# A gated feed-forward stage on one core: up-projection by seven block products, down-projection summed in PSUM

## The chip, the cores and the metric

The kernel runs on one core of a Trainium2 chip. It is written in Bass with the Tile framework, whose scheduler sets the order of instructions on each engine within the limits of data and buffers. The metric is device time in microseconds (us) of one launch; less is better.

Engines are named as in the profile: PE is TensorE (matmul) and PEld its weight loads, DVE is VectorE, ACT is ScalarE, POOL is GpSimd, SP is SyncE, which issues the DMA transfers. PSUM has 8 banks of 128 x 512 f32 here, given out by two tags: "mm" for products and "tp" for transposes (before the change "tp" serves the down-projection too).

## The reference

One layer of a streaming encoder, for a prompt of 1024 rows and 8 samples of 16 rows: 1152 rows of 1024 features, f32. The first sub-layer (adaLN, attention, spatial gating, output projection) stays as it is up to its last projection. The second is the one that changes:

```python
x = x + gt1 * mixed                             # mixed = (...) @ w_out
h2 = modulate(rms_norm(x, norm2_g), sh2, sc2)   # 1152 x 1024
g, u = jnp.split(h2 @ w_ffn_in, 2, axis=-1)     # w_ffn_in 1024 x 5632, D_FF = 2816
gp = jnp.concatenate([conv_cache, g], axis=1)   # two rows ahead of the prompt (zeros) and of each sample
gc = ffn_conv_b
for j in range(3):
    gc = gc + ffn_conv_w[j] * gp[:, j:j + T]    # causal, by feature
out = (jax.nn.gelu(gc) * u) @ w_ffn_out         # 2816 x 1024
x = x + gt2 * out
new_conv = gp[:, -2:]
```

## The kernel before

Each f32 operand of a matmul is kept as two fp32r parts: hi, a rounded copy written by ACT, and lo, the rest, written by DVE or POOL (`split`, L75). A product takes three matmuls for every 128 of the contraction: hi x hi, hi x lo, lo x hi (`mm3`, L97 to L102, so that L100, L101 and L102 are the lines of nearly all matmuls).

**The projection ahead** (`w_out`, L875): two halves of 512 columns, nine token tiles of 128 rows; each product (mxps, 24 matmuls of 512 columns) is gated by DVE (L886) and added to x by POOL (L887). In the second half each tile is written to DRAM (x1_d) and normalised; after tiles 4 and 7 and, later, 8 three tiles are transposed on PE (h2ps), scaled and shifted, and split into h2T, the feature-major operand: 3 chunks of 384 tokens (`h2_chunk`).

**Up** (`up`, L915): 22 feature blocks f of 128. The weights of a block (1024 x 128 of the gate, as much of the up half) come in eight loads to four tiles and are split (wfi). For each chunk of 384 tokens the gate (gps) takes 24 matmuls of 384 columns, ACT copies it out of PSUM into gp, ACT and DVE compute the convolution and the gelu (gc), the up product (ups) takes 24 more, DVE multiplies gc by it, and gc is split into aTh and aTl.

**Down** (`down`, L959): for each f two loads of 128 x 512 of w_ffn_out (wfo), and for each of nine token tiles and two halves three matmuls of 512 columns into one tp bank (fops), which DVE adds to a sum in SBUF (acc, L973). The last two blocks are taken together (`down_last`, flps), with the gate, the addition of x and the output.

The calls are in the order up(f), down(f-1); the scheduler interleaves both on PE. Staging tiles for weights (wst) are five, split weights (wp) nine.

Of the kernel before, what the change touches and what calls it, by code (L numbers as in the profile page):

```python
# [23 lines left out]
NC = TOK // CH  # L24
DB, DS = 8, 16
# [12 lines left out]
def tile_layer(ctx: ExitStack, tc: tile.TileContext, io):  # L38
# [97 lines left out]
    x1_d = dram.tile([TOK, D], F32, name="x1_d")  # L136
    rel_d = dram.tile([H, 512], F32, name="rel_d")
# [691 lines left out]
    psum_phase(3, 5, 0)  # L829
# [14 lines left out]
    with tc.tile_pool(name="mp", bufs=1) as mp_:  # L844
# [17 lines left out]
        g1p, g1s = stile(D, "g1p"), stile(D, "g1s")  # L862
        for j in range(2):
            gate_rows(1, j, g1p[:, 512 * j:512 * (j + 1)], g1s[:, 512 * j:512 * (j + 1)])
        x1 = [stile(D, f"x1_{t}") for t in range(NT)]
        w_o = io["w_out"][0]
        junk2 = stile(D, "junk2")
        h2T = []

        def h2_chunk(c, pl, *tag):  # L870
            for k in range(KD):
                ps = transpose_k(c, k, x1[3 * c:3 * c + 3], "h2")
                modulate(h2T, c, k, ps, G2, S2, pl, "h2", *tag)

        for blk in range(2):  # L875
            bs = slice(512 * blk, 512 * (blk + 1))
            wo = load_block(w_o, 512 * blk, 512, f"wo{blk}")
            if blk == 1:
                h2T = new_xT("h2T")
            for t in range(NT):  # L880
                xr = mp_.tile([P, 512], F32, tag="xr", name=f"xr{blk}_{t}", bufs=3)
                sp.dma_start(xr, xrows(t)[:, bs])
                ps = mmps(f"mxps{blk}_{t}")
                mm_tok(ps, mT, wo, t, 512)
                gt = g1p if t < NTP else g1s
                dve.tensor_tensor(x1[t][:, bs], ps, gt[:, bs], ALU.mult)  # L886
                pool.tensor_tensor(x1[t][:, bs], x1[t][:, bs], xr, ALU.add)  # L887
                if blk == 1:
                    sp.dma_start(x1_d[t * P:(t + 1) * P, :], x1[t])
                    normalise(x1[t], mp_, junk2, f"x1n{t}")  # L890
                    if t in (4, 7):
                        h2_chunk((t - 4) // 3, mp_)


    wfi = io["w_ffn_in"][0].rearrange("r (a n) -> r a n", a=2)
    wfo = io["w_ffn_out"][0]
    with tc.tile_pool(name="fp", bufs=1) as fp:
        acc = [None] * NT
        glast = fp.tile([P, 512], F32, name="glast")
        ccT = fp.tile([P, 3, P], F32, name="ccT")  # L900
# [12 lines left out]
        glv = glast[:, 0:18 * NF].rearrange("p (r f) -> p f r", f=NF)

        def up(f):  # L915
            w = []
# [4 lines left out]
            aT = (stile(TOK, f"aTh{f}", F32R), stile(TOK, f"aTl{f}", F32R))
            w0, w1, w2, bb = convw[:, 0, f:f + 1], convw[:, 1, f:f + 1], convw[:, 2, f:f + 1], convb[:, f:f + 1]
            prev = None
            for c in range(NC):
# [10 lines left out]
                act.activation(gp[:, 2:2 + npr], gps[:, :npr], AF.Copy)  # L935
                gc = fp.tile([P, CH], F32, tag="gc", name=f"gc{f}_{c}", bufs=4)
                parts = [(gp[:, 0:npr], gp[:, 1:npr + 1], gp[:, 2:npr + 2], gc[:, :npr])]
                if npr < CH:
                    sg = gp[:, npr + 2:npr + 2 + DB * 18].rearrange("p (b s) -> p b s", b=DB)
                    act.activation(sg[:, :, 2:18], gps[:, npr:].rearrange("p (b s) -> p b s", b=DB), AF.Copy)  # L940
                    dve.tensor_copy(sg[:, :, 0:2], ccv[:, f, :, :])
                    parts.append((sg[:, :, 0:16], sg[:, :, 1:17], sg[:, :, 2:18], gc[:, npr:].rearrange("p (b s) -> p b s", b=DB)))
                    dve.tensor_copy(glv[:, f, 0:2], gp[:, npr:npr + 2])
# [12 lines left out]
        def load_down(f):
            return [load_w(wfo[f * P:(f + 1) * P, hf * 512:(hf + 1) * 512], [512], f"wfo{f}_{hf}") for hf in range(2)]

        def down(f, aT):  # L959
# [4 lines left out]
            for t in range(NT):
                ts_ = slice(t * P, (t + 1) * P)
                for hf in range(2):
                    hs = slice(512 * hf, 512 * (hf + 1))
                    ps = tpps(f"fops{f}_{t}_{hf}")
                    mm3(ps, [(aT[0][:, ts_], aT[1][:, ts_], w[hf][:, 0, :], w[hf][:, 1, :])])
                    if f == 0:  # L970
                        dve.tensor_copy(acc[t][:, hs], ps)
                    else:
                        dve.tensor_tensor(acc[t][:, hs], ps, acc[t][:, hs], ALU.add)  # L973

        def gate_acc():

            g2 = []
            gpt = stile(D, "g2p")
            for j in range(2):
                gp = gpt[:, 512 * j:512 * (j + 1)]  # L980
                gs = fp.tile([P, 512], F32, name=f"g2s{j}")
# [98 lines left out]
```

## Time and profile before

| | us |
|---|---|
| median of 3 runs (lowest, highest) | 1732.83 (1732.26, 1732.91) |
| the profiled execution: its time | 1734.26 |
| its span, first to last instruction | 1732.5 |
| PE busy in it | 1697.4 |
| DVE, ACT, POOL busy | 934.8, 585.8, 266.5 |
| mean granted clock of PE | 0.994 of full speed |

Busy time counts each instruction from its start to its end, with overlaps counted once. Matmuls overlap: the next one starts before the last has drained, so that the mean duration of one is longer than what it adds to a dense sequence. Idle time is put down to what ended it. Rows of the form "L973 DVE TENSOR_TENSOR acc<-fops,acc 128x512 ... x342" are groups: line, engine, operation, output and inputs, shape, count, then busy time and mean ns of one.

### The profile page before, as it was taken

Reading aid. Unit: us, or ns where it says so; the run is one execution under the profiler, and the core shown is the slowest. Engines: PE = TensorE matmul, PEld = TensorE weight load, DVE = VectorE, ACT = ScalarE, POOL = GpSimd, SP = SyncE. Lnnn points to the kernel's source line nnn. Section 1 sums busy time; section 2 is a strip of 40 time slices with the busy share of each in tenths; the row PEclk is TensorE's granted clock in tenths of the full one; section 3 lists DMA queues with packets and bytes.
Section 4 is the critical chain, followed back from the end, with each engine's and each line's share of the span. In section 5 each row is a group of like instructions: output and inputs, shape, how many; then the busy total and the mean of one; then the engine's idle time right before and its main releaser. Section 6 shows DMA issues by size and latency. Waiting matters only on the chain.

```text
span 1732.5 us, 26462 instructions
## 1 busy us (share of the span) xinstructions
PE 1697.4 (98%) x10244; PEld 1550.0 (89%) x10244; DVE 934.8 (54%) x2011; ACT 585.8 (34%) x1263; POOL 266.5 (15%) x400
## 2 busy tenths in 40 slices
PE   6999999999999999999999999999999999999998
PEld 4798888799998889898889999999999999999997
DVE  4552111137667534472367666556666555666677
ACT  5442111136555534540254222223222223222221
POOL 5410000034224200053351000000000000000063
PEclk9999999999999999999999999999999999999999
DMA  9125444421110133472442111111111111111123
GB/s 352 59 74 165 150 138 142 153 60 33 52 33 17 40 114 106 134 271 72 140 134 66 38 37 42 44 37 45 54 37 37 49 37 37 61 38 37 41 82 150
DMA packets 131090, 147.60 MB, mean 85 GB/s; under 512 B 11544, under 2 KB 101892, under 8 KB 130965
## 3 DMA queue, kind: packets, MB, share of 16 engines
q1 hardware_dynamic: 130965, 145.92, 26.3%
q8 instruction: 80, 1.31, 0.3%
q14 instruction: 45, 0.37, 0.1%
HBM read 123.34 MB, written 24.60 MB: 85 GB/s over the span
## 4 chain that ended last, share of the span: by engine, by line
PE 89%; DVE 4%; DMA 2%; issue 2%; ACT 1%; POOL 1%; DVEq 0%; ACTq 0%; POOLq 0%
PE ups L102 5%; PE ups L100 5%; PE ups L101 5%; PE gps L100 5%; PE gps L102 5%; PE gps L101 5%; PE fops L101 5%; PE fops L100 5%; PE fops L102 5%; PE gbps L102 2%; PE o L686 2%; PE qkps L100 2%; PE gbps L100 2%; PE gbps L101 2%; PE qkps L102 2%; PE qkps L101 2%
## 5 line engine op out<-in xcount | busy, mean ns | idle before, releaser
L973 DVE TENSOR_TENSOR acc<-fops,acc 128x512 f32<-128x512 f32 x342 | 231.7, 687 | 85.1 <-PE fops L102 84.8
L100 PE MATMUL ups<-h2T,wfi 128*128 128x384 f32 x528 | 178.7, 338 | 2.2 <-ACT gp L935 2.2
L101 PE MATMUL ups<-h2T,wfi 128*128 128x384 f32 x528 | 178.3, 338 | 0.0
L102 PE MATMUL ups<-h2T,wfi 128*128 128x384 f32 x528 | 178.2, 337 | 0.0
L102 PE MATMUL gps<-h2T,wfi 128*128 128x384 f32 x528 | 177.3, 336 | 0.4 <-DVE wfi L77 0.4
L100 PE MATMUL gps<-h2T,wfi 128*128 128x384 f32 x528 | 177.4, 336 | 0.0
L101 PE MATMUL gps<-h2T,wfi 128*128 128x384 f32 x528 | 177.0, 335 | 0.0
L935 ACT ACTIVATE gp<-gps 128x384 f32<-128x384 f32 (+1 forms) x66 | 30.1, 456 | 336.2 <-PE gps L102 330.3
L102 PE MATMUL fops<-wfo,aTl 128*128 128x512 f32 x360 | 141.9, 394 | 0.0
L100 PE MATMUL fops<-wfo,aTh 128*128 128x512 f32 x360 | 141.9, 394 | 0.0
L101 PE MATMUL fops<-wfo,aTh 128*128 128x512 f32 x360 | 141.8, 394 | 0.0
L930 POOL MEMSET gp<- 128x2 f32 x22 | 2.1, 99 | 712.7 <-DVE gc L948 712.7
L100 PEld LDWEIGHTS ups<-h2T,wfi 128*128 128x128 f32 x528 | 100.0, 189 | 6.1 <-ACT gp L935 2.5
L102 PEld LDWEIGHTS ups<-h2T,wfi 128*128 128x128 f32 x528 | 99.9, 189 | 5.1
L101 PEld LDWEIGHTS ups<-h2T,wfi 128*128 128x128 f32 x528 | 100.1, 190 | 3.8
L102 PEld LDWEIGHTS gps<-h2T,wfi 128*128 128x128 f32 x528 | 99.2, 188 | 4.4 <-DVE wfi L77 0.8
L100 PEld LDWEIGHTS gps<-h2T,wfi 128*128 128x128 f32 x528 | 99.2, 188 | 3.5
L101 PEld LDWEIGHTS gps<-h2T,wfi 128*128 128x128 f32 x528 | 99.2, 188 | 2.8
L100 PE MATMUL qkps<-wqk,h1T 128*128 128x256 f32 x288 | 83.7, 291 | 0.9 <-ACT qf L580 0.9
L101 PE MATMUL qkps<-wqk,h1T 128*128 128x256 f32 x288 | 82.0, 285 | 0.0
L102 PE MATMUL qkps<-wqk,h1T 128*128 128x256 f32 x288 | 81.9, 284 | 0.0
L102 PEld LDWEIGHTS fops<-wfo,aTl 128*128 128x128 f32 x360 | 67.6, 188 | 15.9
(416 smaller groups left out, 4072.3 us busy)
## 6 DMA issues: line engine op xcount, KB each, us to landing
adaw<-in_w_ada_dram SPq DMA_DIRECT2D x48, 512.0 KB, 4.9
wfi_0s<-in_w_ffn_in_dram SPq DMA_DIRECT2D x44, 128.0 KB, 2.5
wfi_1s<-in_w_ffn_in_dram SPq DMA_DIRECT2D x44, 128.0 KB, 2.7
wfi_2s<-in_w_ffn_in_dram SPq DMA_DIRECT2D x44, 128.0 KB, 2.6
wfi_3s<-in_w_ffn_in_dram SPq DMA_DIRECT2D x44, 128.0 KB, 2.7
wfo_0s<-in_w_ffn_out_dram SPq DMA_DIRECT2D x22, 256.0 KB, 3.2
wfo_1s<-in_w_ffn_out_dram SPq DMA_DIRECT2D x22, 256.0 KB
mb_d<-sgb SPq DMA_DIRECT2D x8, 576.0 KB, 4.2
```

What stands on the lines that cost most here:

```text
L100: pe.matmul(ps, lhsT=ah, rhs=bh, start=(i == 0), stop=False)
L101: pe.matmul(ps, lhsT=ah, rhs=bl, start=False, stop=False)
L102: pe.matmul(ps, lhsT=al, rhs=bh, start=False, stop=(i == n - 1))
L686: pe.matmul(o[hs, :], lhsT=v[:, k0 // P + i, hs], rhs=out[t, x][:, i * P:(i + 1) * P], start=(i == 0), stop=(i == nk - 1))
L930: pool.memset(gp[:, 0:2], 0.0)
L935: act.activation(gp[:, 2:2 + npr], gps[:, :npr], AF.Copy)
L973: dve.tensor_tensor(acc[t][:, hs], ps, acc[t][:, hs], ALU.add)
```

## The change

With the rows of h2 in four blocks of 288 tokens (QB) and the 1024 features of the contraction in two halves, a unit u is two token blocks (a = 2u, b = 2u + 1). The product of a 2 x 2 block matrix of h2 (token block by half of the contraction) and one of the weights (half by gate or up column) is formed from seven block products and not eight (Winograd's form of Strassen's algorithm). Each block product is 4 k x 3 = 12 matmuls of 288 columns:

- operands of a unit: A11, A12, A22 and S1 = A21 + A22, S2 = S1 - A11, S3 = A11 - A21, S4 = A12 - S2;
- weights of a feature block: B11, B21, B22 and T1 = B12 - B11, T2 = B22 - T1, T3 = B22 - B12, T4 = B21 - T2;
- products: A11 B11, S2 T2, S3 T3 and A22 T4 accumulate one after the other in bank X, A12 B21 in Y, S1 T1 and then S4 B22 in Z. ACT copies X out after the first, second, third and fourth product; DVE adds what belongs together.

All operands (7 x 2 units x 4 k, hi and lo) are built before the up stage by `operands`: unit 0 behind token tile 4 of w_out's second half, unit 1 after tile 8. `raw_block` makes a transposed, scaled and shifted block of 288 tokens, alternately on ACT and DVE. POOL and DVE form the sums, ACT and DVE the splits. The weights of each f are loaded in four transfers of 256 KB; POOL forms the T sums, and seven tiles are split where four were.

The gated result is not split and kept, but written to DRAM (aT_d, four transfers for each f). Down is a stage after up: three groups of three token tiles, whose six sums of 128 x 512 stay in six PSUM banks over all 22 f. For every f the group loads and splits a 128 x 384 piece of aT_d and both wfo tiles, so that wfo is loaded three times in all. At a group's end DVE multiplies the banks by the gate, adds x1 (read from DRAM) and SP writes them out. After the attention stage PSUM is given out as six mm banks and two tp banks; it was three and five. The rows xr that w_out adds share the five staging tiles of the weights.

```diff
-    psum_phase(3, 5, 0)
+    psum_phase(6, 2, 0)
...
+    def operands(u, first):
+        at = Slices(u)
+        for k in range(4):
+            a11, a12 = first[k], first[k + 4]
+            a21, a22 = (raw_block(2 * u + 1, kk, "r") for kk in (k, k + 4))
+            s1, s2, s3, s4 = (vtile(f"s{i}_{u}_{k}") for i in range(1, 5))
+            pool.tensor_tensor(s1, a21, a22, ALU.add)
+            dve.tensor_tensor(s2, s1, a11, ALU.subtract)
+            pool.tensor_tensor(s3, a11, a21, ALU.subtract)
+            dve.tensor_tensor(s4, a12, s2, ALU.subtract)
+            for op, src in zip(OPS, (a11, a12, a22, s1, s2, s3, s4)):
+                hi, lo = at.take(), at.take()
+                split(hi, lo, src)
+                opnd[u][op, k] = (hi, lo)
...
+                if t in (2, 6):
+                    first[t // 4] = [raw_block(0 if t == 2 else 2, k, "a") for k in range(KD)]
+                if t == 4:
+                    operands(0, first[0])
...
+        pool.tensor_tensor(t3, b22, b12, ALU.subtract)
+        pool.tensor_tensor(b12, b12, b11, ALU.subtract)
...
+        pool.tensor_tensor(t2, b22, t1, ALU.subtract)
...
+        pool.tensor_tensor(b21, b21, t2, ALU.subtract)
...
+    def unit(f, u, W):
+        ca, cb = 2 * u, 2 * u + 1
+        X, Y, Z = (mmps(f"{n}{f}_{u}", QB) for n in "XYZ")
+        product(X, u, "A11", W["B11"], True)
+        act.activation(x1c, X, AF.Copy)
...
+        product(Y, u, "A12", W["B21"], True)
...
+            dve.tensor_tensor(dst, y, x, ALU.add)
...
+        gca = conv(f, ca, *gate_rows_in(f, ca, sum_in))
...
+        product(X, u, "S2", W["T2"], False)
+        act.activation(u2, X, AF.Copy)
...
+        product(Z, u, "S1", W["T1"], True)
...
+        product(X, u, "S3", W["T3"], False)
+        act.activation(u3, X, AF.Copy)
+        dve.tensor_tensor(upb, Z, u3, ALU.add)
...
+        product(X, u, "A22", W["T4"], False)
...
+        gcb = conv(f, cb, *gate_rows_in(f, cb, copy_in))
+        gated(f, cb, gcb, upb)
...
+        product(Z, u, "S4", W["B22"], False)
+        dve.tensor_tensor(u2, Z, u2, ALU.add)
+        gated(f, ca, gca, u2)
...
+    for g in range(3):
+        ts = range(3 * g, 3 * g + 3)
+        acc = {(t, hf): mmps(f"fops{t}_{hf}") for t in ts for hf in range(2)}
+        for f in range(NF):
+            a = load_w(aT_d[f][:, g * CH:(g + 1) * CH], [CH], f"a{g}_{f}")
+            w = [load_w(wfo[f * P:(f + 1) * P, hf * 512:(hf + 1) * 512], [512], f"wfo{g}_{f}_{hf}") for hf in range(2)]
...
+                        pe.matmul(acc[t, hf], lhsT=a[:, x, o], rhs=w[hf][:, y, :], start=(f == 0 and i == 0), stop=(f == NF - 1 and i == 2))
```

Three places show how the change moves instructions. The first is DVE around the last token tile of w_out (x1_8). Before, weight splits (wfi, L77), one chunk of scaled rows (h2t) and then the first convolution stand there:

```order
L245 TENSOR_SCALAR h2t1_6_9197<-h2ps1_6_9193,G2_83,S2_84 128x384 [waits PE_49,Pool_49]
L77 TENSOR_TENSOR wfi1_1_9358<-wfi1_1s_9355,wfi1_1_9358 128x512 [waits DMAHW1_49,Activation_49]
L886 TENSOR_TENSOR x1_8_8444<-mxps1_8_9211,g1s_8417 128x512 [waits PE_49]
L245 TENSOR_SCALAR h2t1_7_9205<-h2ps1_7_9201,G2_83,S2_84 128x384 [waits Pool_49]
L77 TENSOR_TENSOR wfi1_2_9364<-wfi1_2s_9361,wfi1_2_9364 128x512 [waits DMAHW1_49,DMAHW0_49,Activation_49]
```

After, the rows from x1_8 on are operand splits (L78, op) and sums (s2, s4):

```order
L959 TENSOR_TENSOR x1_8_8472<-mxps1_8_9345,g1s_8445 128x512 [waits PE_49]
L78 TENSOR_TENSOR wB21_0_9401<-b0_10_9394,wB21_0_9401 128x512 [waits DMAHW1_49,Activation_49]
L78 TENSOR_TENSOR op10_9074<-s3_0_0_9057,op10_9074 128x288 [waits Activation_49]
L78 TENSOR_TENSOR op10_9074<-s4_0_0_9058,op10_9074 128x288 [waits Activation_49]
L78 TENSOR_TENSOR op10_9074<-r1_5_9089,op10_9074 128x288 [waits Activation_49]
L935 TENSOR_TENSOR s2_0_1_9092<-s1_0_1_9091,a0_1_8933 128x288 [waits Pool_49]
L937 TENSOR_TENSOR s4_0_1_9094<-a0_5_8957,s2_0_1_9092 128x288 [waits DVE_49]
L919 TENSOR_SCALAR r1_2_9119<-h2ps1_2_9115,G2_83,S2_84 128x288 [waits PE_49]
```

Some hundred rows follow from x1_8 to the sum of Y0_0 (L1083), most of them splits of op.

The second place is PE in the middle of the up stage, feature block 10. Before, one up product follows the gate product, and its first matmul waits for ACT (X_49 in brackets is the semaphore of engine X):

```order
L102 MATMUL gps10_1_12498<-h2T01_8788,wfi10_3_12432 128x384
L100 MATMUL ups10_1_12531<-h2T01_8788,wfi10_0_12414 128x384 [waits Activation_49]
L101 MATMUL ups10_1_12531<-h2T11_8791,wfi10_0_12414 128x384
L102 MATMUL ups10_1_12531<-h2T01_8788,wfi10_0_12414 128x384
L100 MATMUL ups10_1_12531<-h2T01_8788,wfi10_0_12414 128x384
```

After, S3's product into X10_0 (weights wT3) is followed by ten matmuls into X11_0, and A22's product (wT4) goes to the same bank X10_0:

```order
L1028 MATMUL X10_0_12284<-op10_9074,wT3_10_12247 128x288 [waits Activation_49]
L1028 MATMUL X10_0_12284<-op10_9074,wT3_10_12247 128x288 x2
L1028 MATMUL X10_0_12284<-op0_2_9110,wT3_10_12247 128x288 x3
L1028 MATMUL X10_0_12284<-op01_9145,wT3_10_12247 128x288 x3
L1028 MATMUL X10_0_12284<-op11_9176,wT3_10_12247 128x288 x3
L1028 MATMUL X11_0_12558<-op00_9063,wB11_11_12399 128x288
L1028 MATMUL X11_0_12558<-op10_9074,wB11_11_12399 128x288 x3
L1028 MATMUL X11_0_12558<-op0_3_9135,wB11_11_12399 128x288 x3
L1028 MATMUL X11_0_12558<-op01_9145,wB11_11_12399 128x288 x3
L1028 MATMUL X10_0_12284<-op00_9063,wT4_10_12262 128x288 [waits Activation_49]
L1028 MATMUL X10_0_12284<-op00_9063,wT4_10_12262 128x288 x2
```

A bank of one unit is thus written four times, with an ACT copy between, and other units' matmuls stand between.

The third place is SP, which issues the loads. Before, the two wfo loads of a block stand between the loads of wfi for the following ones:

```order
L90 DMA wfi16_3s_14325<-in_w_ffn_in_dram 128x2x128 [waits DMAHW6_49,DVE_49]
L90 DMA wfi16_3s_14325<-in_w_ffn_in_dram 128x2x128 [waits DMAHW7_49]
L92 DMA wfo15_0s_14523<-in_w_ffn_out_dram 128x512 [waits DMAHW0_49,DVE_49]
L92 DMA wfo15_1s_14528<-in_w_ffn_out_dram 128x512 [waits DMAHW1_49,DVE_49]
L90 DMA wfi17_0s_14623<-in_w_ffn_in_dram 128x2x128 [waits DMAHW3_49,DMAHW2_49,DVE_49]
```

After, at the passage from up to down, the writes of the last gated rows (gc to aT_d) and of the convolution's rows (glo) stand between the first loads of the down stage:

```order
L1067 DMA aT_d21_110<-gc21_1_15453 128x288 [waits DMAHW7_49,DVE_49]
L1067 DMA aT_d21_110<-gc21_0_15359 128x288 [waits DMAHW0_49,DVE_49]
L93 DMA a0_0s_15619<-aT_d0_89 128x384 [waits DMAHW1_49,Activation_49,Pool_49]
L93 DMA wfo0_0_0s_15624<-in_w_ffn_out_dram 128x512 [waits DMAHW2_49,Activation_49]
L93 DMA wfo0_0_1s_15629<-in_w_ffn_out_dram 128x512 [waits DMAHW3_49,Activation_49,Pool_49]
L1125 DMA o_cp_dram<-glo_15586 44x128 [waits DMAHW4_49,DVE_49]
L1067 DMA aT_d21_110<-gc21_2_15475 128x288 [waits DMAHW5_49,DVE_49]
L1067 DMA aT_d21_110<-gc21_3_15556 128x288 [waits DMAHW6_49,DVE_49]
L1126 DMA o_cs_dram<-glo_15586 84x128 [waits DMAHW7_49]
L1129 DMA o_cs_dram<-glo_15586 128x128 [waits DMAHW0_49]
L1129 DMA o_cs_dram<-glo_15586 128x128 [waits DMAHW1_49]
L1129 DMA o_cs_dram<-glo_15586 12x128 [waits DMAHW2_49]
```

The second load from aT_d (a0_1s) comes in the next row.

More of the change, by code (lines that the diff above doesn't have):

```diff
@@ L24 @@
 NC = TOK // CH
+QB = TOK // 4
 DB, DS = 8, 16
@@ L136, in tile_layer @@
     x1_d = dram.tile([TOK, D], F32, name="x1_d")
+    aT_d = [dram.tile([P, TOK], F32, name=f"aT_d{f}") for f in range(NF)]
     rel_d = dram.tile([H, 512], F32, name="rel_d")
@@ L860, in tile_layer @@
                 split(mT[0][c][:, j, :], mT[1][c][:, j, :], m)
[L862 to L873, printed above, removed]
@@ L875, in tile_layer @@
-        for blk in range(2):
-            bs = slice(512 * blk, 512 * (blk + 1))
-            wo = load_block(w_o, 512 * blk, 512, f"wo{blk}")
-            if blk == 1:
[L879 to L892, printed above, removed]
@@ new lines, in tile_layer @@
+    g1p, g1s = stile(D, "g1p"), stile(D, "g1s")
+    for j in range(2):
+        gate_rows(1, j, g1p[:, 512 * j:512 * (j + 1)], g1s[:, 512 * j:512 * (j + 1)])
+    x1 = [stile(D, f"x1_{t}") for t in range(NT)]
+    w_o = io["w_out"][0]
+    junk2 = stile(D, "junk2")
+    first = [None, None]
+    for blk in range(2):
+        bs = slice(512 * blk, 512 * (blk + 1))
+        wo = load_block(w_o, 512 * blk, 512, f"wo{blk}")
+        for t in range(NT):
+            xr = staged(f"xr{blk}_{t}")
+            sp.dma_start(xr, xrows(t)[:, bs])
+            ps = mmps(f"mxps{blk}_{t}")
+            mm_tok(ps, mT, wo, t, 512)
+            gt = g1p if t < NTP else g1s
+            dve.tensor_tensor(x1[t][:, bs], ps, gt[:, bs], ALU.mult)
+            pool.tensor_tensor(x1[t][:, bs], x1[t][:, bs], xr, ALU.add)
+            if blk == 1:
+                sp.dma_start(x1_d[t * P:(t + 1) * P, :], x1[t])
+                normalise(x1[t], fp, junk2, f"x1n{t}")
+                if t in (2, 6):
+                    first[t // 4] = [raw_block(0 if t == 2 else 2, k, "a") for k in range(KD)]
+                if t == 4:
+                    operands(0, first[0])
@@ new lines, in product, with gate_rows_in @@
+    def product(ps, u, op, w, begin):
+        n = 0
+        for k in range(4):
+            hi, lo = opnd[u][op, k]
+            ks = slice(k * P, (k + 1) * P)
+            for wj, x in ((0, hi), (0, lo), (1, hi)):
+                pe.matmul(ps, lhsT=w[:, wj, ks], rhs=x, start=(begin and n == 0), stop=(n == 11), skip_group_check=True)
+                n += 1
+    halo = [None]
+    def gate_rows_in(f, c, fill):
+        gp = vtile(f"gp{f}_{c}", NV)
+        if c == 0:
+            pool.memset(gp[:, 0:2], 0.0)
+        else:
+            pool.tensor_copy(gp[:, 0:2], halo[0][:, QB:QB + 2])
+        halo[0] = gp
+        npr = min(QB, SEQ - c * QB)
+        fill(gp[:, 2:2 + npr], 0, npr)
+        sg = None
+        if npr < QB:
+            sg = gp[:, npr + 2:npr + 2 + DB * 18].rearrange("p (b s) -> p b s", b=DB)
+            fill(sg[:, :, 2:18], npr, QB)
+            dve.tensor_copy(sg[:, :, 0:2], ccv[:, f, :, :])
+            dve.tensor_copy(glv[:, f, 0:2], gp[:, npr:npr + 2])
+            dve.tensor_copy(glv[:, f, 2:18].rearrange("p (b j) -> p b j", b=DB), sg[:, :, 16:18])
+        return gp, sg, npr
@@ new lines, in tile_layer @@
+    W = [{} for _ in range(NF)]
+    ws = [up_weights(f, W[f]) for f in range(NF)]
+    for _ in range(2):
+        next(ws[0])
+    operands(1, first[1])
+    for g in ws[0]:
+        pass
+    prev = None
+    for f in range(NF):
+        nxt = ws[f + 1] if f + 1 < NF else iter(())
+        for u in range(2):
+            g = unit(f, u, W[f])
+            for i in range(5):
+                next(g)
+                if prev is not None and i < 2:
+                    next(prev)
+                if u == 1 or i >= 3:
+                    next(nxt, None)
+            prev = g
```

303 lines of the change are left out of this document (159 added, 144 removed).

## The prediction, made before the changed kernel had run

> **What bounds the kernel now.** I read the page first (span, busy shares, the chain of waits), then the timeline of TensorE, its groups by form, and the span cut at the places where TensorE's order changes.
>
> ```profile
> span 1732.5 us, 26462 instructions
> PE 1697.4 (98%) x10244; PEld 1550.0 (89%) x10244; DVE 934.8 (54%) x2011; ACT 585.8 (34%) x1263; POOL 266.5 (15%) x400
> PE 89%; DVE 4%; DMA 2%; issue 2%; ACT 1%; POOL 1%; DVEq 0%; ACTq 0%; POOLq 0%
> ```
>
> TensorE is busy for 98% and carries 89% of the chain that ends last; the other engines have half of their time free. So the price of a matmul decides. Its price is not its duration, since matmuls overlap. The timeline (start, duration) gives it from start to start:
>
> ```profile
> 401.82 0.28 PE L101 MATMUL qkps<-wqk,h1T 128*128 128x256 f32 x1
> 404.45 0.28 PE L102 MATMUL qkps<-wqk,h1T 128*128 128x256 f32 x1
> 841.76 0.39 PE L100 MATMUL mxps<-wo,mT 128*128 128x512 f32 x1
> 847.20 0.39 PE L100 MATMUL mxps<-wo,mT 128*128 128x512 f32 x1
> 911.61 1.25 PE L234 MATMUL h2ps<-ident,x 128*128 128x128 f32 x10
> 1202.19 0.33 PE L100 MATMUL gps<-h2T,wfi 128*128 128x384 f32 x1
> 1206.35 0.34 PE L100 MATMUL ups<-h2T,wfi 128*128 128x384 f32 x1
> ```
>
> The two qkps rows stand 22 matmuls apart: 2.63/22 = 0.1195 us for 256 columns. The mxps rows are 24 apart: 5.44/24 = 0.2267 for 512. The last two are 24 apart: 4.16/24 = 0.1733 for 384. Ten transposes take 1.25, the last of them about 0.27, so 0.109 each. Between 256 and 384 the line gives 0.133 for the new width of 288, which no row has.
>
> ```profile
> 785.30:888.70 103.40, 103.40 (x482) 86.30 (x481) 38.56 (x53) 25.19 (x47) 39.00 (x43) 1.00 0.33 108
> 900.90:903.90 3.00, 0.79 (x4) 0.47 (x3) 0.92 (x2) 0.87 (x2) 0.41 (x4) 0.91 0.77 212
> 903.90:911.00 7.10, 6.50 (x24) 5.83 (x24) 4.30 (x9) 4.26 (x7) 0.00 (x0) 0.56 0.34 85
> 911.00:1683.00 772.00, 772.00 (x4090) 724.64 (x4089) 484.00 (x904) 220.14 (x420) 28.84 (x38) 1.00 0.15 45
> 1683.00:1726.80 43.80, 41.73 (x205) 36.25 (x203) 37.98 (x56) 6.98 (x14) 20.20 (x15) 1.00 0.37 137
> 1726.80:1732.50 5.70, 0.00 (x0) 0.00 (x0) 2.79 (x5) 0.00 (x0) 0.00 (x0) 0.73 0.46 184
> ```
>
> These are busy times and counts by stretch (PE, weight loads, DVE, ACT, POOL, then the granted clock). TensorE is full up to 900.9; then it waits some 2.2 us, runs about 7 us at a granted clock of 0.56, is full again from 911, and leaves a tail of 5.7 after its last matmul. The counts show what is not dense. From 785.3 to 1726.8 (941.5 us) the code issues 3168 matmuls of 384 columns, 432 + 1188 of 512, 79 transposes and 3 last ones of the stage ahead: 549.0 + 367.3 + 8.6 + 0.5 = 925.4 us. So 16 us there are no dense work: 5 at 900.9 to 911, about 2 of idle time after 1683, the rest spread over the alternation of widths.
>
> **The change, part by part.**
>
> *Up-projection.* 3168 x 0.1733 = 549.0 us become 22 x 2 x 7 x 12 = 3696 x 0.133 = 491.6: -57.4. The Trainium skill ("TensorE: Matmul & The Clock Gate", section "Back-to-back issue gap") gives an isolated gap of N/2.4 + 2.5 ns; by it the two would be 514.8 and 452.8, an estimate of -62. The rows, 11 to 13 ns above that gap, decide here.
>
> *Down-projection.* The same 1188 matmuls of 512: nothing. Its 342 adds into acc go, which are not on the path.
>
> ```profile
> L973 DVE TENSOR_TENSOR acc<-fops,acc 128x512 f32<-128x512 f32 x342 | 231.7, 687 | 85.1 <-PE fops L102 84.8
> ```
>
> *Transposes* of the normalised rows: 96 instead of 72 (blocks of 288 rows out of three tiles of 128): 24 x 0.109 = +2.6.
>
> *The losses of before* go with the order that made them and are counted anew below: -14 of the 16 (some may be rounding of the spacings, and 7 are shown idle time).
>
> *Building the operands* is the new work on the path. Each of the 7 operands exists for 2 units and 4 k: 56 splits of 288 into hi (ACT) and lo (DVE), 16 sums on DVE, 16 on POOL. The unit-1 part can start only when the last token tile is normalised.
>
> ```profile
> 1211.41 0.69 DVE L973 TENSOR_TENSOR acc<-fops,acc 128x512 f32<-128x512 f32 x1
> 1212.01 0.68 DVE L77 TENSOR_TENSOR wfi<-wfi_0s,wfi 128x512 fp32r<-128x512 f32 x1
> 1212.61 0.69 DVE L973 TENSOR_TENSOR acc<-fops,acc 128x512 f32<-128x512 f32 x1
> L77 DVE TENSOR_TENSOR aTl<-gc,aTh 128x384 fp32r<-128x384 f32 x66 | 37.2, 563 | 25.4 <-ACT aTh L76 25.4
> 835.25 1.29 POOL L887 TENSOR_TENSOR x<-x,xr 128x512 f32<-128x512 f32 x1 [4.14 <-DVE x L886]
> 835.67 1.43 DVE L77 TENSOR_TENSOR wo<-wo_6s,wo 128x512 fp32r<-128x512 f32 x1 [0.49 <-ACT wo L76]
> L593 POOL TENSOR_TENSOR qk<-qk,kg 128x128 f32<-128x128 f32 x36 | 17.6, 488 | 25.3 <-DVE qk L591 12.7 <-issue 3.7 <-ACT qf L580 3.4
> ```
>
> DVE works 512 columns every 0.60 us (1211.41, 1212.01, 1212.61) with 0.69 for one; 384 take 0.563 alone, so 0.13 less, and 288 about 0.37 apart by the same slope. POOL takes 0.488 for 128 and 1.29 for 512, so 0.82 for 288. In DVE's order after the change a hundred rows stand between the end of the last w_out product and the point from which TensorE has all it needs: 47 splits and 14 sums of 288 (61 x 0.37 = 22.6), 10 weight splits (6.0), and 29 of other kinds (block rows out of PSUM, the last normalise, the sample's rows, the first sum of Y: about 9): 38 us. POOL has 14 sums of 288 and 8 of 512 there, and two small ones: 23.8. The two meet: at 835.67 a split that otherwise takes 0.69 took 1.43 while POOL ran 1.29, 0.57 us lost per us of POOL, so 23.8 x 0.57 = 13.6. DVE also waits in its order for POOL's first sum and ACT's copies at each of 8 steps (0.8 us, one sum, each): 6. That makes 58 us. TensorE has other work for 17.3 of them: six products of f = 0 (72 x 0.133 = 9.6), 22 sets of three transposes (7.2), the transposes of the cache rows (0.5). Loss 58 - 17.3 = 41, and after such a gap the half clock of 903.9 to 911 comes again (24 matmuls in 7.1 instead of 4.2): +3. Together +44. The bounds: 38 us (nothing meets, no waits) gives +24; 75 (POOL wholly in series, 62, and twice the waits) gives +61. I take 58, which rests on the row at 835.67.
>
> The Trainium skill ("SBUF — State Buffer", section "Who interferes with whom") states that a DVE instruction with two SBUF inputs contends with a GpSimd instruction that reads SBUF, through a shared pair that is an exclusive lock. By that rule alone the two times add up, 38 + 24 = 62; the row at 835.67, held up for 0.74 of POOL's 1.29, agrees in kind.
>
> *The steady up stage.* A feature block is 168 x 0.133 = 22.3 us.
>
> ```profile
> L76 ACT ACTIVATE wfo<-wfo_1s 128x512 fp32r<-128x512 f32 x22 | 13.9, 633 | 2.5 <-PE fops L102 2.5
> L935 ACT ACTIVATE gp<-gps 128x384 f32<-128x384 f32 x44 | 21.6, 492 | 270.5 <-PE gps L102 264.7 <-issue 5.8
> L935 ACT ACTIVATE gp<-gps 128x256 f32<-128x256 f32 x22 | 8.5, 384 | 65.6 <-PE gps L102 65.6
> 1206.54 0.38 ACT L935 ACTIVATE gp<-gps 128x256 f32<-128x256 f32 x1 [2.97 <-PE gps L102]
> ```
>
> ACT has 7 weight splits (7 x 0.633), 9 copies out of PSUM (0.41, between 0.384 and 0.492) and 4 conv and gelu pairs: some 12.5 us of 22.3. DVE has the same 7 splits, about 8 conv steps and 10 adds: 14 to 16. Both fit, so throughput costs nothing. New is that X is handed to ACT and taken back three times in each unit. In the order, S3's product into X10_0 is followed by 10 matmuls of another bank (1.33 us), and then A22's product needs X10_0 copied. ACT starts a copy at once when free (1206.54, while the last gps matmul, started at 1206.17, ends at 1206.50): 0.33 for the matmul's end, 0.41 copy, about 0.2 to let go: 0.96 of 1.33. With a weight split (0.63) just begun it is 1.6, late by 0.25. Some such delays in 22 blocks: +5, and +3 for the first blocks after the build. Bounds: 0 and 1 us per block (22). I take the lower side, since the order puts other work ahead of each such wait.
>
> *Up to down.* The first loads of the down stage stand on SP behind the writes of gc21_1 and gc21_0, the second step's behind those of gc21_2, gc21_3 and the cache rows.
>
> ```profile
> wfo_0s<-in_w_ffn_out_dram SPq DMA_DIRECT2D x22, 256.0 KB, 3.2
> o_yp_dram<-acc SPq DMA_DIRECT2D x8, 512.0 KB, 2.6
> GB/s 352 59 74 165 150 138 142 153 60 33 52 33 17 40 114 106 134 271 72 140 134 66 38 37 42 44 37 45 54 37 37 49 37 37 61 38 37 41 82 150
> ```
>
> A load lands 3.2 us after its issue, then a split by ACT (0.63) and DVE (0.69): 4.5 behind the write's issue, of which the last products hide a part: +3 (0 to 8). After that each f of a group of three token tiles has 18 x 0.2267 = 4.08 us of matmuls, for which 0.7 MB must come, 173 GB/s; slices of this trace reached 271 and 352. Five staging buffers at three per step must each be refilled within 5 x 4.08/3 = 6.8 us: 3.2 + 1.3 + the queue, near 5.5. So +3 for three group starts (0 to 10). The gated rows' 88 writes and 22 more pairs of weight loads run on queues that are idle there. Tail: 12 DVE steps and a write as now; 5.7 stays.
>
> **Sum.** -57.4 + 2.6 - 14 + 44 + 8 + 6 = -10.8. The profiled execution took 1734.3 (its span 1732.5 and 1.8 around it), so 1723.5; the median of the runs, 1732.83, is 1.4 below that execution, so 1722.
>
> **Rivals.**
>
> 1. *Hand-overs of X, Y and Z* (the slower side). If ACT or DVE are late at most of the 12 waits of a feature block, each by 0.1 us, a block loses 1.2 instead of 0.2: +22, 1744. From 0.9 us per block (1722 + 22 x 0.67 = 1737) the kernel is slower. For it: three copies in series on one bank, and DVE behind POOL's weight sums; against it: ACT's 44% free. Chance 0.2.
> 2. *The build is better hidden* (38 us instead of 58): 1702, chance 0.12; or *worse* (75): 1739, chance 0.1. For the first, most of POOL's sums may fall where DVE waits anyway; for the second, the split of 1.43 is one instance and queues wait in order.
> 3. *The down stage goes by its loads.* If a refill takes 7.5 instead of 6.8 us, a step takes 4.5: 66 x 0.4 = +26, 1748. For it: loads share queues with the x1 rows; against: 173 GB/s is half of what the first slice moved. Chance 0.08.
> 4. *Narrow matmuls don't get cheaper*, because each one's weight load must fit in:
>
> ```profile
> L101 PEld LDWEIGHTS qkps<-wqk,h1T 128*128 128x128 f32 x288 | 55.1, 191 | 0.3 <-issue 0.2
> ```
>
> A weight load takes 0.191, longer than 0.133; if it set the pace, 3696 x 0.191 = 706, and the kernel would take 1936. But beside that same load the qkps matmuls run every 0.1195. Chance 0.02. The Trainium skill, in the section named first, also says that in a stream of such pairs the spacing is set by both, 81 ns at 128 columns and 131 at 512; between these, as an estimate, 3696 narrow matmuls would cost 14 us more than 3168 wide ones. By that rule the change loses; the mxps rows, 227 ns at 512, contradict it.
>
> **How the numbers follow.** The forecast has 0.48, with a range of its own of 1712 to 1733. A measurement can tell 0.2%, 3.5 us: faster is under 1729.4, slower over 1736.3. Faster: 0.41 of the forecast and 0.12 of the better build, 0.53. Same: 0.07 of the forecast and 0.07 from the near ends of rivals 1 and 2: 0.14. Slower: 0.33. The range from 1704 to 1747 leaves out the far end of the better build, the down stage by its loads, and the narrow matmuls.
>
> **What would show it.** Products in the trace 0.133 us apart; TensorE idle for about 40 us between the last mxps and the second product of unit 1, with DVE full and its 288-column splits near 0.7 while POOL runs; up blocks at 22.5 us; fops 0.2267 apart for 269 us, with less than 1 us at a group's start. Wrong would be the forecast with up blocks above 23.2, with gaps before fops at each f that end with a load, or with an idle stretch under 25 or over 55 us.

## The result

The changed kernel takes 1714.82 us (median of 4 runs, 1712.86 to 1715.73) where the kernel before takes 1732.87 in the same runs: 18.0 us less, ratio 0.9893 with a 95% interval of 0.9876 to 0.991. The profiled execution took 1715.73 with a span of 1714.0, 18.5 below the span before.

The page of the changed kernel, the rows that answer to those of before:

```profile
span 1714.0 us, 28905 instructions
PE 1652.3 (96%) x10796; PEld 1502.5 (88%) x10796; DVE 918.7 (54%) x2013; ACT 721.2 (42%) x1613; POOL 357.5 (21%) x526
PE 89%; DVE 4%; DMA 2%; POOL 1%; ACT 1%; issue 1%; SPq 0%; DVEq 0%; POOLq 0%; ACTq 0%
```

TensorE still carries 89% of the chain. The span cut at the new stages (PE, weight loads, DVE, ACT, POOL, granted clock, DMA):

```profile
786.60:888.40 101.80, 101.80 (x466) 84.24 (x465) 35.12 (x53) 21.47 (x41) 32.82 (x39) 1.00 0.35 111
888.40:945.00 56.60, 30.54 (x139) 23.69 (x137) 48.81 (x97) 28.59 (x68) 30.30 (x26) 0.65 0.14 44
945.00:955.00 10.00, 8.16 (x44) 7.60 (x45) 6.65 (x14) 6.37 (x13) 1.60 (x3) 0.74 0.27 79
955.00:1410.00 455.00, 455.00 (x3437) 455.00 (x3436) 317.18 (x611) 221.92 (x510) 121.67 (x163) 1.00 0.24 73
1410.00:1432.10 22.10, 20.60 (x152) 19.90 (x151) 10.02 (x30) 8.67 (x23) 0.49 (x3) 1.00 0.32 97
1432.10:1442.00 9.90, 7.03 (x24) 4.97 (x23) 5.04 (x12) 3.53 (x7) 0.00 (x0) 0.83 0.51 153
1442.00:1707.10 265.10, 265.09 (x1170) 219.21 (x1168) 137.14 (x224) 108.45 (x193) 0.00 (x0) 1.00 0.64 202
1707.10:1714.00 6.90, 0.00 (x0) 0.00 (x0) 4.00 (x7) 0.00 (x0) 0.00 (x0) 0.82 0.51 197
```

Three things are to be seen. From 955 to 1410 the up stage is dense: 455.00/3437 = 0.1324 us for a matmul of 288 columns. From 1442 to 1707 the down stage is dense too, at 202 GB/s. And between the last w_out product (888.3) and 955 TensorE does little, while DVE is busy for 48.8 of 56.6 us. With each matmul and transpose counted at its dense spacing (0.2267, 0.1324, 0.109 us), TensorE loses 44.3 us from 888.3 to 960, 0.2 from there to 1400, 7.6 from 1400 to 1450, at the passage, and 0.1 in the rest of the down stage. In the kernel before it lost 6.1 where the up stage began and 10.4 behind that.

In the build two waits belong together. The timeline of POOL, DVE and PE (start, duration, idle time ahead and what ended it):

```profile
930.53 4.36 POOL L1004 TENSOR_TENSOR t<-b,b 128x512 f32<-128x512 f32 x1 [5.65 <-DMA b<-in_w_ffn_in_dram]
930.98 0.68 DVE L78 TENSOR_TENSOR wB<-b,wB 128x512 fp32r<-128x512 f32 x1
931.78 0.45 DVE L78 TENSOR_TENSOR op<-s,op 128x288 fp32r<-128x288 f32 x1
934.97 1.26 POOL L1005 TENSOR_TENSOR b<-b,b 128x512 f32<-128x512 f32 x1
936.31 1.26 POOL L1009 TENSOR_TENSOR t<-b,b 128x512 f32<-128x512 f32 x1
937.53 0.79 POOL L934 TENSOR_TENSOR s<-r,r 128x288 f32<-128x288 f32 x1
938.28 1.27 POOL L1013 TENSOR_TENSOR b<-b,t 128x512 f32<-128x512 f32 x1
938.35 1.51 DVE L935 TENSOR_TENSOR s<-s,a 128x288 f32<-128x288 f32 x1 [4.58 <-POOL s L934]
938.85 0.61 PE L1028 MATMUL Z<-op,wT 128*128 128x288 f32 x1 [7.21 <-ACT op L77]
```

POOL takes up three weight sums of the next feature block (L1004, L1005, L1009) ahead of an operand sum (L934). The first of them is held for 4.36 us instead of 1.29 while DVE works through its splits. Then DVE waits 4.58 for the operand sum, and TensorE 7.21 for ACT's split of it. The Trainium skill ("SBUF — State Buffer", section "Who interferes with whom") says that issue order decides which of the two blocks. The rows agree only in part. The sum on DVE at 938.35, which starts behind POOL's of 938.28, took 1.51, where splits of the same size take 0.45. But DVE's splits at 930.98 and 931.78 start behind POOL's sum of 930.53, and they keep their usual 0.68 and 0.45.

### The profile page after: what moved, and what is told of

Read it like the earlier page. It is cut to its first block, busy times and chain, and to the rows that moved or that the text cites. A ratio compares the mean times of both kernels' runs of the same rounds, so it can differ in the third digit from the quotient of the medians.

```text
span 1714.0 us, 28905 instructions
## 1 busy us (share of the span) xinstructions
PE 1652.3 (96%) x10796; PEld 1502.5 (88%) x10796; DVE 918.7 (54%) x2013; ACT 721.2 (42%) x1613; POOL 357.5 (21%) x526
## 4 chain that ended last, share of the span: by engine, by line
PE 89%; DVE 4%; DMA 2%; POOL 1%; ACT 1%; issue 1%; SPq 0%; DVEq 0%; POOLq 0%; ACTq 0%
PE X L1028 16%; PE fops L1170 15%; PE Z L1028 8%; PE Y L1028 4%; PE o L688 2%; PE gbps L103 2%; PE qkps L101 2%; PE gbps L101 2%; PE gbps L102 2%; PE qkps L103 2%; PE qkps L102 2%; PE gaps L101 2%; PE gaps L102 2%; PE gaps L103 2%; PE adaps L382 2%; PE ptp L678 2%
## 5 line engine op out<-in xcount | busy, mean ns | idle before, releaser
L1170 PE MATMUL fops<-wfo,a 128*128 128x512 f32 x1188 | 271.7, 391 | 2.9 <-ACT wfo L77 2.9
L1170 PEld LDWEIGHTS fops<-wfo,a 128*128 128x128 f32 x1188 | 224.0, 189 | 50.4 <-ACT wfo L77 3.9
L1028 PE MATMUL X<-op,wT 128*128 128x288 f32 x1584 | 233.3, 296 | 2.0 <-ACT u L1095 1.5
L1028 PEld LDWEIGHTS X<-op,wT 128*128 128x128 f32 x1584 | 218.7, 189 | 2.9 <-ACT u L1095 2.2
L1028 PE MATMUL Z<-op,wT 128*128 128x288 f32 x528 | 79.8, 298 | 11.0 <-ACT op L77 8.2
L1028 PE MATMUL X<-op,wB 128*128 128x288 f32 x528 | 83.8, 300 | 1.9 <-DVE op L78 1.9
L1028 PE MATMUL Y<-op,wB 128*128 128x288 f32 x528 | 80.3, 299 | 0.2
L1028 PE MATMUL Z<-op,wB 128*128 128x288 f32 x528 | 77.0, 294 | 0.0
L1004 POOL TENSOR_TENSOR t<-b,b 128x512 f32<-128x512 f32 x22 | 31.4, 1428 | 191.0 <-DVE wB L78 177.7
L101 PE MATMUL gaps<-h1T,wga 128*128 128x384 f32 x192 | 66.6, 347 | 0.0
L103 PE MATMUL gbps<-h1T,wgb 128*128 128x384 f32 x192 | 65.9, 343 | 0.0
L102 PE MATMUL gaps<-h1T,wga 128*128 128x384 f32 x192 | 65.1, 339 | 0.0
L101 PE MATMUL gbps<-h1T,wgb 128*128 128x384 f32 x192 | 64.9, 338 | 0.0
```

What stands on the lines that cost most here:

```text
L101: pe.matmul(ps, lhsT=ah, rhs=bh, start=(i == 0), stop=False)
L102: pe.matmul(ps, lhsT=ah, rhs=bl, start=False, stop=False)
L103: pe.matmul(ps, lhsT=al, rhs=bh, start=False, stop=(i == n - 1))
L1004: pool.tensor_tensor(t3, b22, b12, ALU.subtract)
L1028: pe.matmul(ps, lhsT=w[:, wj, ks], rhs=x, start=(begin and n == 0), stop=(n == 11), skip_group_check=True)
L1170: pe.matmul(acc[t, hf], lhsT=a[:, x, o], rhs=w[hf][:, y, :], start=(f == 0 and i == 0), stop=(f == NF - 1 and i == 2))
```

## The experiments

Each kernel ran in turns with the kernel before, so ratios to it are compared. Losses are TensorE's, counted as above.

**The down stage alone (e1).** The up-projection of before, with the new down stage:

```diff
-                split(aT[0][:, cs], aT[1][:, cs], gc)
+                sp.dma_start(aT_d[f][:, cs], gc)
...
+        for f in range(2, NF):
+            run(up(f))
         conv_rows()
+        psum_phase(6, 2, 0)
```

> The up-projection of before (eight block products' worth, 384 columns), its gated rows written to DRAM, and the new down stage behind it. Theory (the seven products gain 60 us and their operands give back about 44; the down stage by itself matters little): before's loss of 16 us beside dense work shrinks by the alternation of widths and the idle time at its end, some 9, and 3.5 at the passage and 1.2 in the tail come new: 1728 us, -3 to -8. Rival (the gain of the change comes from the down stage, from its sums in PSUM and the adds that go): -15 to -18, 1715 to 1718.

Measured: 1723.12 beside 1735.44, ratio 0.9931 (0.9916 to 0.9946), 12 us less. The cut of its span:

```profile
892.90:960.00 67.10, 66.99 (x397) 66.57 (x396) 39.28 (x82) 28.73 (x54) 12.69 (x18) 1.00 0.30 92
960.00:1441.00 481.00, 481.00 (x2777) 481.00 (x2776) 167.43 (x383) 146.67 (x287) 1.79 (x18) 1.00 0.21 66
1441.00:1448.00 7.00, 5.87 (x34) 5.47 (x33) 5.18 (x12) 4.16 (x9) 0.00 (x0) 1.00 0.35 93
1448.00:1716.60 268.60, 268.58 (x1185) 222.11 (x1183) 134.32 (x219) 106.38 (x189) 0.00 (x0) 1.00 0.62 196
1716.60:1723.70 7.10, 0.00 (x0) 0.00 (x0) 3.98 (x7) 0.00 (x0) 0.00 (x0) 0.74 0.50 191
```

It fell between the two expectations. Of the 16.5 us that the kernel before loses 2.0 are left, most of them new, at the passage to the down stage. The idle time where its up stage begins (6.1) is gone as well, which I had left standing. So about two thirds of the gain of the change is the separate down stage. The seven products, with their operands, are worth the rest, 0.9931 to 0.9893, some 7 us (3 to 11 by the two intervals). e1 changes the order, the sums in PSUM and the way through DRAM all at once; that the order alone makes its gain, since nothing is interleaved any more, is my reading and wasn't tested apart.

**The price of the operands (e3).** S1 to S4 and their splits are left out, so that the gated rows are not the reference's:

```diff
-            for op, src in zip(OPS, (a11, a12, a22, s1, s2, s3, s4)):
+            for op, src in zip(OPS, (a11, a12, a22)):
...
+            for op, o in (("S1", "A22"), ("S2", "A11"), ("S3", "A11"), ("S4", "A12")):
+                opnd[u][op, k] = opnd[u][o, k]
```

> The operand sums S1 to S4 and their splits are left out; the products read the splits of A11, A12 and A22 in their place, so that all matmuls stay. Theory (the build is DVE's work): after the last w_out product some 27 splits and 14 sums of 0.37 fall out of DVE's order (15 us), with POOL's hold-ups (7) and the waits for POOL's sums (5): -25, 1690 us, dense from about 922 instead of 947. Rival (the chain of the last tile, its transposes and PSUM banks sets the end of the build): -5 to -10, 1705 to 1710.

Measured: 1682.26 beside 1735.44, ratio 0.9693 (0.9679 to 0.9708). The loss of the build falls from 44.3 to 13.3, and dense work begins near 920:

```profile
885.00:920.00 35.00, 28.24 (x179) 23.75 (x177) 30.78 (x57) 21.41 (x45) 13.20 (x13) 0.90 0.38 106
920.00:960.00 40.00, 40.00 (x303) 40.00 (x303) 28.32 (x54) 20.18 (x46) 11.71 (x15) 1.00 0.26 76
```

So 31 us of the build are the sums and their splits, on all engines together, more than the 25 expected; the transposes, the other splits and the last tile's chain leave no more than 13.

**Sums on DVE (e2).**

```diff
-            pool.tensor_tensor(s1, a21, a22, ALU.add)
+            dve.tensor_tensor(s1, a21, a22, ALU.add)
...
-            pool.tensor_tensor(s3, a11, a21, ALU.subtract)
+            dve.tensor_tensor(s3, a11, a21, ALU.subtract)
```

> The changed kernel with the operand sums S1 and S3 formed on DVE, as S2 and S4 are; POOL forms only the sums of the weights. Theory (DVE loses by POOL's reads and by waiting for POOL's sums in its order): DVE gets some 12 more rows of 0.37 us after the last w_out product, +4.5, and loses the hold-ups by 14 POOL sums (14 x 0.9 x 0.57 = 7) and the waits for POOL (4.6 + 0.7): -8, 1707 us, TensorE dense about 8 us earlier. Rival (the number of DVE's rows decides alone): +4.5, 1719 us.

Measured: 1709.36 beside 1735.44, ratio 0.9844 (0.9826 to 0.9862); the loss of the build is 39.6. Against the changed kernel's 0.9893 that is 0.005, some 8.5 us, as the theory gave; 4.7 of it can be placed in the build by the two profiled executions, the rest can't. More rows on DVE, and less time: POOL's part cost more than it took off DVE.

**A third bank for transposes (e4).**

```diff
-    psum_phase(6, 2, 0)
+    psum_phase(5, 3, 0)
...
     conv_rows()
+    psum_phase(6, 2, 0)
```

> Three PSUM banks for transposes and five for products up to the end of the up stage, instead of two and six; the down stage with six as it is. Theory (TensorE's waits at the transposes, 14 us in the list of waits, only show how late DVE and ACT are): within 2 us in the build, and no more than 3 us lost by the fifth bank: 1712 to 1718 us. Rival (the two banks hold up the build): -8 to -14, 1701 to 1707 us.

Measured: 1708.12 beside 1735.44, ratio 0.9841 (0.9826 to 0.9855), the size that the rival gave. The loss of the build is 36.8; five banks cost the up stage nothing (0.3 from 960 to 1400). The waits of DVE in the build, of the changed kernel first and of this one second:

```profile
DVE s L935 <- POOL s L934: 5.3, 2, 4.6
```

```profile
DVE s L935 <- POOL s L934: 0.7, 1, 0.7
```

The list of TensorE's waits at the transposes is hardly shorter (9.6 us at L923 alone). But POOL's first weight sum, which waits for the transposes of the cache rows, starts at 905.5 instead of 912.9, and DVE hardly waits for POOL's sum any more. Two causes are mixed here, the bank and the order.

**Both, and rows on ACT (e9, e10).** e9 has the edits of e2 and e4 together. In e10 ACT also makes all the rows out of PSUM:

```diff
-        if k % 2:
+        if True:
             act.activation(t[:, :npr], x[:, :npr], AF.Identity, bias=S2[:, k, 0:1], scale=G2[:, k, 0:1])
...
-    dve.tensor_copy(ccT, ps[:, 0:3 * P].rearrange("p (a b) -> p a b", a=3))
+    act.activation(ccT, ps[:, 0:3 * P].rearrange("p (a b) -> p a b", a=3), AF.Copy)
```

> The third transpose bank (five for products) and the operand sums on DVE together. If the third bank gained 7 us of build because transposes came earlier, the two add up: loss of the build 44.3 - 4.7 - 7.5 = 32, -17 against the changed kernel as it is, ratio to before 0.979. If it gained only because another order of POOL took away DVE's wait of 4.6 us for POOL's sum, which the sums on DVE take away as well: 39, ratio 0.984.

> As the last, and ACT, not DVE, scales and shifts all the transposed rows and copies the cache rows. If the number of DVE's rows bounds the build: ten or so rows out of PSUM of 0.49 us leave DVE after the last w_out product, 5 us less loss than the last, ratio 0.976. If ACT, whose copies stand ahead of each DVE split, is by then as late as DVE: no gain or a loss of up to 3 us, 0.979 to 0.981.

Measured: e9 1706.94 beside 1735.59, ratio 0.9831 (0.9816 to 0.9846), loss of the build 35.2; e10 1706.72, ratio 0.9838 (0.9823 to 0.9852), loss 35.7. By the ratios the two edits of e9 mostly overlap: e2 gains 8.5 us on the changed kernel, e4 9.0, both together 10.7. The losses of the build overlap less, 4.7, 7.5 and 9.1 us below 44.3, each from one profiled execution. So it fits that the third bank gained in the main by taking away DVE's wait for POOL, but it isn't shown. The build of e9, then of e10:

```profile
888.00:918.00 30.00, 20.31 (x108) 17.33 (x107) 29.54 (x65) 17.78 (x41) 10.33 (x10) 0.77 0.26 80
918.00:945.00 27.00, 13.70 (x63) 11.13 (x61) 23.50 (x51) 14.36 (x32) 6.42 (x6) 0.68 0.16 49
```

```profile
888.00:918.00 30.00, 20.48 (x95) 16.66 (x94) 25.32 (x52) 22.30 (x52) 9.31 (x10) 0.73 0.25 76
918.00:945.00 27.00, 14.97 (x74) 12.84 (x73) 23.25 (x51) 15.11 (x34) 6.43 (x6) 0.66 0.19 56
```

In e9 DVE is busy for 29.5 of the first 30 us: nothing is left there but its rows. In e10 it has 13 rows less and 25.3 us, but then it waits for ACT's copies (4.5 us in five waits), and the end stays.

**More work beside the build (e5, e6, e7, e11).** Two orders were tried: e5 brings unit 0's rows earlier, e6 moves unit 1 of block 0 to the end. e7 has the edits of e5, e6 and e2 together, e11 those of e10 and e6. The lines that set the orders in e5 and in e6:

```diff
-    for blk in range(2):
+    for part, (blk, tiles) in enumerate(((0, range(5)), (1, range(NT)), (0, range(5, NT)))):
...
```

```diff
+    groups = [(f, (0,), W[f], ws[f]) for f in SPLIT]
+    groups += [(f, (0, 1), W[f], ws[f]) for f in range(NF) if f not in SPLIT]
+    groups += [(f, (1,), w, up_weights(f, w)) for f, w in zip(SPLIT, W2)]
...
```

> The changed kernel with another order of the w_out projection: first half for token tiles 0 to 4, second half for all nine, first half for tiles 5 to 8 (its weights loaded and split a second time). Unit 0's rows are complete after 10 of 18 products instead of 14. Theory (the build is DVE work, and what is done beside the projection is free): DVE gets 22 us more beside w_out, pays 8 weight splits (4.8): some 40 rows leave the stretch after the last product, -12 to -17, 1698 to 1703 us. Rival (only the chain from the last tile to unit 1 decides): 0 to +3, 1715 to 1718 us.

> The changed kernel with unit 1 of feature block 0 done last of all, its weights loaded, summed and split a second time; so six products of feature block 1 on unit 0 stand ahead of the first one that needs unit 1's operands. Theory (TensorE lacks work in the build): 84 x 0.1324 = 11.1 us of work move into the wait, DVE has up to 4 more weight splits in it (2.4) and POOL none more: -8, 1707 us; the second set of weights at the end costs nothing. Rival (block 1's weights come no earlier than unit 1's operands, since DVE and POOL make both): 0 to -3, 1712 to 1715 us.

> The order of tiles, the order of units and the operand sums on DVE together. If the three take from the same wait of DVE's work and are worth 8 (measured), 12 to 17 and 8 by themselves, the loss of the build falls from 44 to about 12: -30, 1685 us. If they overlap, since TensorE then has work for most of the time that DVE needs: -20, 1695 us.

> As the last, with unit 1 of feature block 0 done last of all. Alone that change gained nothing, since block 1's weights came too late from DVE and POOL. If DVE is now freer, part of the 11 us of products on unit 0 falls into the wait: -5, ratio 0.973; if the weights are still late: 0.

Measured: e5 1714.89 beside 1732.09, ratio 0.99 (0.9882 to 0.9919); e6 1714.36, ratio 0.9902 (0.9879 to 0.9926); e7 1707.93, ratio 0.9859 (0.984 to 0.9877), no better than e2 alone; e11 1708.59 beside 1735.59, ratio 0.9844 (0.9828 to 0.9861), no better than e10. My expectations of a gain from e5, e6 and e7 all failed, and of the two outcomes for e11 the one without a gain came. In e5 the loss behind the last w_out product falls only to 39.6, and up to there, from the stage ahead of w_out on, TensorE now loses 4.8 instead of 2.2. DVE, meant to use the time beside the projection, waits in its order for the weight splits of w_out and for transposes that stand behind products on TensorE (waits between 840 and 900):

```profile
DVE a L919 <- PE h2ps L912: 10.2, 4, 3.5
DVE wo L78 <- ACT wo L77: 6.2, 3, 3.9
```

In e6 the products of block 1 come no earlier, because their weights don't. POOL waits for their loads, and TensorE for the splits that follow (first row of TensorE below). In the second row it waits for a copy of X, which stands behind operand splits in ACT's order and starts at 942.81:

```profile
POOL t L1004 <- DMA b<-in_w_ffn_in_dram: 14.8, 2, 9.1
```

```profile
936.28 2.77 PE L1028 MATMUL Z<-op,wT 128*128 128x288 f32 x10 [2.32 <-DVE wT L78]
943.26 3.25 PE L1028 MATMUL X<-op,wT 128*128 128x288 f32 x12 [4.21 <-ACT x1c L1079]
```

**The hand-over of X (e8).** Each of the three copies is made twice, so that X comes free later:

```diff
         act.activation(x1c, X, AF.Copy)
+        act.activation(x1c, X, AF.Copy)
...
         act.activation(u2, X, AF.Copy)
+        act.activation(u2, X, AF.Copy)
...
         act.activation(u3, X, AF.Copy)
+        act.activation(u3, X, AF.Copy)
```

> The changed kernel, in which ACT copies bank X out twice after the first, second and third product (the same copy again), so that X comes free about 0.32 us later, 6 times in a feature block. Theory (ten matmuls, 1.32 us, stand behind a product of X; 0.33 for the last matmul's end, 0.41 for the copy and some 0.1 are needed, so 0.4 to 0.5 is spare): 0 to +3 us, 1715 to 1718. Rival (the hand-over is hidden only just): 132 x 0.3 = +40 at most, over +10 in any case: 1725 to 1755 us.

Measured: 1755.55 beside 1732.09, ratio 1.0133 (1.0111 to 1.0155): 41 us more than the changed kernel. The rival's size, but not its mechanism. In the steady blocks one hand-over in each waits 1.4 us (19 of the 22 waits in the row below, which counts from 980 to 1500; the other three are of 0.9, in the last block), and the other five wait for nothing. Counted from start to start it costs more than the idle time: such products start at 1208.27 and 1232.24, so a block takes 24.0 us instead of 22.2. ACT and PE at one of them:

```profile
PE X L1028 <- ACT u L1098: 30.1, 22, 1.4
```

```profile
1206.46 0.41 ACT L1097 ACTIVATE u<-X 128x288 f32<-128x288 f32 x1 [4.06 <-PE X L1028]
1206.77 1.14 ACT L77 ACTIVATE wB<-b 128x512 fp32r<-128x512 f32 x2
1207.81 0.40 ACT L1098 ACTIVATE u<-X 128x288 f32<-128x288 f32 x1
```

```profile
1206.27 0.56 PE L1028 MATMUL X<-op,wB 128*128 128x288 f32 x3
1208.27 1.86 PE L1028 MATMUL X<-op,wT 128*128 128x288 f32 x12 [1.44 <-ACT u L1098]
```

The second copy stands behind two weight splits in ACT's order, and only three matmuls of another bank stand on TensorE where ten stood: the second copy has also changed the order of TensorE. In the same trace the copy made twice costs nothing where nine or more matmuls stand between. So in these runs the place in two orders, not 0.3 us of copy, decides a hand-over.

## Why the prediction came out right, and where not

The forecast was -10.8 against the profiled execution and 1722 us; measured -18.5 in the spans and 1714.82 us, inside the range of 1704 to 1747 and inside the forecast's own 1712 to 1733, near its lower end. By its terms, with what the two traces show:

| term | predicted | measured |
|---|---|---|
| up matmuls, 3696 x 0.133 | -57.4 | -59.6 (0.1324) |
| transposes | +2.6 | +2.6, by count |
| losses of before | -14 | -16.5 (6.1 and 10.4) |
| build of the operands, with the half clock | +44 | +44.3 |
| first blocks and steady up stage | +8 | +0.2 |
| passage to down, starts of groups | +6 | +7.7 |
| tail | 0 | +1.2 |
| start of the stage ahead of w_out | 0 | +1.6 |
| sum | -10.8 | -18.5 |

- *The build* was right in size, and its reason, DVE's rows with POOL in their way, is borne out by e3 and e2. From the last w_out product (888.3) to the start of dense work (947.6) it took 59.3 us, where 58 were forecast. In part that was luck. DVE's rows there took some 12 us more than the shortest of their kind, where 13.6 were forecast. But POOL, held itself, was busy for 30.3 us and not 23.8, and cost DVE about 0.40 us for each us and not 0.57, so that two misses cancel. The waits of DVE for POOL and ACT were put at 0.8 us in each of eight steps; for POOL it was 5.3 us in two waits, one of them of 4.6, behind weight sums that I had in POOL's list but not in its order.
- *The steady up stage* is the term that was mis-sized: 8 us where nothing was lost. I let some copies be late behind a weight split on average; in the order that was built each hand-over fitted, every time. One hand-over was put at 0.96 us, with 0.2 in it to let the bank go that no row showed; at the bare ones the copy's end (1420.67) and the next matmul (1420.72) are 0.05 apart, and the whole takes 0.79. e8 shows how near rival 1 was all the same: one more copy, and one place in each block cost 1.4 us.
- *The losses of before* were 16.5, all of which went. I had set 2 of them down to rounding.
- *Rival 2* in either direction didn't come: neither 38 us of DVE nor 75, but 59.3. *Rival 3* is out by the down stage's 265.09 busy in 265.10 us at 202 GB/s (the 0.7 MB of a step are 0.72, so 177 GB/s were needed, not 173). *Rival 4* is out by twelve matmuls in 1.59 us:

```profile
1192.77 1.75 PE L1028 MATMUL Y<-op,wB 128*128 128x288 f32 x12
1194.36 1.75 PE L1028 MATMUL Z<-op,wT 128*128 128x288 f32 x12
```

  The Trainium skill ("TensorE: Matmul & The Clock Gate", section "Back-to-back issue gap") gives for 288 columns, as estimates worked out from its figures, 122.5 ns by its formula for an isolated matmul and 102 by its two sustained figures; the trace has 132.4, above both. (The rows of before lie 10 to 11 ns above that formula, not 11 to 13 as the prediction says; its sum went by the rows.)
- The passage: two loads wait behind the writes, as foreseen (2.08 and 0.78 us). Not foreseen were three bare hand-overs of X at the very end, where no other unit's products are left to stand between:

```profile
1420.72 3.21 PE L1028 MATMUL X<-op,wT 128*128 128x288 f32 x22 [0.50 <-ACT u L1095]
1434.59 6.21 PE L1170 MATMUL fops<-wfo,a 128*128 128x512 f32 x18 [2.08 <-ACT wfo L77]
1441.58 1.66 PE L1170 MATMUL fops<-wfo,a 128*128 128x512 f32 x6 [0.78 <-ACT wfo L77]
```

The fastest version tried is e9, ratio 0.9831 (0.9816 to 0.9846), some 10 us below the changed kernel; e2, e4, e10 and e11 can't be told from it.

What stays open: why the stage ahead of w_out begins 1.6 us later (in the other executions it began between 731.7 and 737.4, so it is as likely spread as cause); how e4's gain divides between the bank and POOL's order; and which part of e1's edit takes away the loss of before, its 6.1 us at the start of the up stage above all.

## What to carry to other kernels

A product form that saves an eighth of the matmuls saves it only net of its operands: here 60 us came off TensorE, and 44 went into a stretch in which TensorE waited mostly for sums and splits (31 of the 44, by e3). The data for half of them came last, and neither order tried in e5 and e6 covered them. Ask first at which moment the last input of the new operands is ready, and count the in-order rows of the slowest engine from there. And try a simplification that rides along by itself: here the separate down stage alone gave some two thirds of the gain.

## What the runs showed of the hardware

- A bare hand-over of a PSUM bank, from TensorE to ACT and back, leaves TensorE idle for 0.50 us with an ACT copy of 288 columns (0.41) in it; from the last matmul's start to the next one's start it is 0.79.
- DVE can hold POOL for longer than POOL holds DVE: one POOL sum of 512 took 4.36 us instead of 1.29 (4.32 in e5 and in e6, at the same place), while the longest DVE row of 288 beside POOL took 1.5 instead of 0.45.
- In the build, where TensorE is only partly busy, the granted clock goes up and down: at half from 896 to 912, back at full by 928, when TensorE had been busy throughout the 4 us before, and at half again later on:

```profile
900.00:904.00 4.00, 3.67 (x15) 3.33 (x16) 3.67 (x10) 2.01 (x5) 0.52 (x1) 0.50 0.00 0
924.00:928.00 4.00, 4.00 (x24) 4.00 (x24) 4.00 (x9) 2.41 (x6) 0.89 (x1) 0.70 0.65 190
928.00:932.00 4.00, 3.05 (x18) 2.06 (x17) 4.00 (x12) 0.96 (x2) 1.47 (x1) 1.00 0.43 135
948.00:952.00 4.00, 4.00 (x24) 4.00 (x23) 2.89 (x7) 2.48 (x4) 0.95 (x1) 0.71 0.60 172
952.00:956.00 4.00, 3.50 (x27) 3.27 (x26) 0.82 (x2) 1.46 (x4) 0.00 (x0) 1.00 0.06 17
```

  The last time it came back some 3 us after dense work had begun (947.6). The first 12 matmuls of that work took 2.80 us instead of 1.59, which is 1.2 us more. What the slow ones before them cost wasn't measured; it should be little, since DVE set the end there.
